# A two-layer decoder trunk on one core: new order of the mixer's steps, token halves in turn at the head of the first feed forward, and the S5 phase tables built on another engine

## The chip, the cores and the metric

The kernel runs on one core of a Trainium2 chip. The metric is the device time of the program in microseconds (us), the median over runs. The engines are named as in the profile: PE (TensorE matmuls; PEld its weight loads), DVE (VectorE), ACT (ScalarE), POOL (GpSimd), SP (SyncE, which here only issues transfers).

## The reference, cut to what matters

```python
D_MODEL, SEQ, D_FF = 1024, 1024, 4096          # one batch, float32
for i in range(2):
    h = h + mix_fns[i](rms_norm(h, norm_mix[i]), *mix_params[i])   # 0: RWKV-7 + short conv, 1: S5
    h = h + sqrelu_mlp(rms_norm(h, norm_ffn[i]), *ffn[i])          # square(relu(hn @ up)) @ down
    gate = jax.nn.sigmoid(rms_norm(h, norm_ple[i]) @ ple[i][0])
    h = h + (p[i] @ ple[i][1]) * gate
return rms_norm(h, norm_final)

# S5 (layer 1): 64 groups of 16 channels, 64 complex states a group
step = exp(log_step)[:, None]; lam_bar = exp(lam * step)           # lam complex
b_bar = ((lam_bar - 1) / lam)[..., None] * (b_re + 1j * b_im)
# h_t = lam_bar * h_(t-1) + b_bar u_t ;  y_t = Re(c h_t) + d_skip * u_t, then gelu and a GLU
```

The kernel's S5 works on chunks of tokens, so it needs powers of `lam_bar` up to 127 (the "phases", real and imaginary part, 128 states x 128 powers for each pair of groups) and products of powers with `b_bar` and `c`.

## The kernel before, in words

All activations are held transposed: 8 blocks `j` of 128 model dimensions by 1024 tokens, the tokens in two halves `hf` of 512. Every float32 product is made of three matmuls (`mm3`, L162 to L164): each operand is split into a rounded high part and the rest (`whi`/`wlo` and `uwh`/`uwl` for weights, `prh`/`prl` for inputs, `hidh`/`hidl` for hidden values), and PE adds high x high, low x high and high x low.

The stages follow each other: mixer 0 (0 to 721 us in the profiled execution), a passage to feed forward 0 (721 to 770), feed forward 0 (to 1490), the per-layer embedding (to 1614), S5 with its GLU (to 1905), feed forward 1 (to 2580), embedding and last norm (to 2722).

**Order.** PE runs in the order in which the program is written. The other engines' order is set by a scheduler from the same program, so an instruction moved in the code can move other engines' rows too. SP issues nearly all weight loads in its own order; a store placed there stands between two loads.

**Mixer 0** (`mixer0_run`, `go`). Short chains with little work per step (`f` the projections' elementwise part with `ps_w`, `ps_a`; `a`, `c` and `g` the recurrence in chunks, with `ps_Kt`, `ps_Bt`, `ps_Vt`, `ps_u`, and its output `ps_yt`) are advanced by a step, and between the steps `go` places units of long matmul work: `z` (input projection), `C` (convolution), `W` (output projection, `ps_wo`), `X` (inputs of the second half). `MIX_STEPS`, `MIX_UNITS` and `MIX_JOBS` are the tables that set who runs when. A chain's step is marked by a `yield`.

**Passage.** `done(j, hf)` splits an input tile into `prh` (ACT, L179) and `prl` (DVE, L180) and squares it for the norm (ACT `sq`, POOL `acc` L201); the norm's scale is made by `ps_ms`, a root, a reciprocal (L222) and `ps_rs`. All 16 inputs are issued ahead of feed forward 0.

**Feed forward** (`ffn`). A block `k` has 8 steps; `at(k, s, f)` puts a function at a step. In a block PE runs a down product in seven parts (`d_run`, a Strassen-like scheme with outputs `ps_dnx`, `ps_dny`, `ps_dnz`) and one up weight tile (`u_run`). `FFN_D` and `FFN_U` say at which steps of a block the weights are loaded and split: for down weights, POOL makes four sums (`draw`, L276 to L279), ACT the high part (`whi`), DVE the rest (`wlo`, L286); for up weights, ACT makes `uwh` (L260) and POOL `uwl` (L263). The raw tiles `uraw` and `draw` share two buffers. DVE adds each product to `h` or `ha` (L360). The eight up tiles of input rows j 0 to 3 and j 4 to 7 alternate (`q, b = m // 2 % 2, m % 2`).

**S5 tables under feed forward 0** (`hook`). While PE works on blocks 1 to 60, `s5_piece` makes for each of 32 pairs of groups `CL` (three POOL instructions), `BL` (three DVE instructions), two PE transposes `ps_bl`, four PE matmuls `ps_k`, and stores them; `CL`, `tmp`, `BL` and `tmp3` share one tag of four buffers (`s5b`). `s5_phases` builds the phases by doubling: seven steps, each with scaled copies on ACT (L1170) and two POOL instructions (L1171, L1172), for two pairs at a time, and POOL issues the stores (L1176).

Of the kernel before, what the change touches and what calls it, by code (L numbers as in the profile page):

```python
# [12 lines left out]
P = 128  # L13
# [7 lines left out]
S5_START, S5_PREP, S5_AT, S5_EACH = -38, 2, 36, 14  # L21
S5_FRONT = (-20, -6, -4, -3)
S5_STEPS = (0, 2, 4, 7, 10)
S5_PH = (1, 5, 9, 13, 17, 21, 25)
# [3 lines left out]
FFN_D = (0, 0, 3, 7)  # L28
# [4 lines left out]
MIX_STEPS = [14, 14, 5, 6, 8]  # L33
MIX_UNITS = [19, 48, 64, 72, 72, 48, 40, 48, 40, 40, 24]
MIX_JOBS = ['z1 C0', 'z2 C1 W45a', 'z3 C2 X3', 'N M L z4 W01a', 'z5 C4', 'z6 W23a', 'z7 C5 S', 'R C6 W45b', 'W01b C7', 'W2b W67b W3b', '']
# [25 lines left out]
class Trunk:  # L61
# [175 lines left out]
    def ffn(self, l, xn, rstd, done, hook):  # L237
# [12 lines left out]

        def u_load(m):
            c, q, b = m // 4, m // 2 % 2, m % 2
# [35 lines left out]
        def u_run(k):  # L288
# [302 lines left out]
    def rwkv_f(self, st, p, cx):  # L591
# [16 lines left out]
        nc.vector.tensor_tensor_scan(L, self.reset, sw, 0.0, ALU.mult, ALU.add)  # L608
        ps = self.pc.tile([P, H], F32, tag="a", name="ps_a")
# [28 lines left out]
    def rwkv_a(self, st, p, cx):  # L638
# [15 lines left out]
        nc.vector.scalar_tensor_tensor(RA[:, 1], v8(kk), -1.0, eL[:, :, 0:64], ALU.mult, ALU.mult)  # L654
        yield
# [40 lines left out]
    def rwkv_c(self, p, cx):  # L696
# [22 lines left out]
        self.by_token(flat(kb[:, 0]), K, "Kt")  # L719
        self.by_token(flat(kb[:, 1]), B, "Bt")  # L720
# [57 lines left out]
    def rwkv_g(self, p, cx, out):  # L778
# [20 lines left out]
        yield  # L799
# [84 lines left out]
    def s5_tables(self, pool, sp, keep_p):  # L884
# [125 lines left out]
        self.Fi = t("Fi", (2, 64), sp)  # L1010
# [6 lines left out]
        stt(self.Fi[:, 0], u, sgn, inv, MUL)  # L1017
        V.tensor_scalar_mul(self.Fi[:, 1], self.Fi[:, 0], -1.0)
# [47 lines left out]
    def s5_front(self, n, pool):  # L1066
# [37 lines left out]
    def s5_piece(self, pc, pool):
# [9 lines left out]
        X, Bb, sk = self.eight  # L1114
# [35 lines left out]
        G.tensor_add(kt[:, :, 112:128], kt[:, :, 112:128], sk[:, q])  # L1150
# [4 lines left out]
        nc.scalar.dma_start(dst, kt.rearrange("p g k -> p (g k)"))  # L1155
        yield

    def s5_phases(self, pc, pool):
# [3 lines left out]
        E = pool.tile([P, 2, 2, P], F32, tag="s5p", name="phase", bufs=1)  # L1162
        G.memset(E[:, :, 0, 0:1], 1.0)
        G.memset(E[:, :, 1, 0:1], 0.0)
        for k in range(7):
            m = 1 << k
            t = pool.tile([P, 2, 2, 64], F32, tag="s5q", name="pt", bufs=1)
            for j in range(2):
                for o, n in ((E[:, j, :, m:2 * m], 0), (t[:, j, :, :m], 1)):
                    nc.scalar.activation(o, E[:, j, :, 0:m], AF.Copy, scale=self.wk[:, k, n, pc + j:pc + j + 1])  # L1170
            G.tensor_sub(E[:, :, 0, m:2 * m], E[:, :, 0, m:2 * m], t[:, :, 1, :m])  # L1171
            G.tensor_add(E[:, :, 1, m:2 * m], E[:, :, 1, m:2 * m], t[:, :, 0, :m])  # L1172
            if k > 0:
                yield
        for j in range(2):
# [536 lines left out]
```

## Time and profile before

| | us |
|---|---|
| median of 3 runs (lowest, highest) | 2727.71 (2727.67, 2731.49) |
| the profiled execution | 2723.54 |
| its span, first to last instruction | 2721.8 |

| engine | busy us | share of the span |
|---|---|---|
| PE | 2571.1 | 94% |
| DVE | 1860.5 | 68% |
| ACT | 1078.4 | 40% |
| POOL | 1140.2 | 42% |

The shares are means over stages with different limits: a wait counts only where PE, the engine that is busy nearly all the time, waits behind it. The mean granted clock of PE was 0.982 of full speed. A matmul of 128x512 columns starts 0.23 us after the one before it at full clock and 0.43 us where the clock is at its lower level, though each one's own duration reads longer since they overlap.

### The profile page before, as it was taken

What the parts mean: (1) busy time and instruction counts of PE and PEld (TensorE: products, weight loads), DVE (VectorE), ACT (ScalarE), POOL (GpSimd) and SP (SyncE); (2) the same over time, 40 slices, a digit from 0 to 9 for tenths busy, and PEclk for the clock granted to TensorE, in tenths of its full rate; (3) what the DMA queues carried; (4) which work ended last, traced back from release to release, by engine and by line L of the source; (5) the groups of instructions that cost most, each with busy time, mean ns of one, the idle gap of its engine ahead of it and who ended that gap; (6) DMA issues with size and microseconds to landing.
All of it is one profiled execution on the core that took longest, in us unless ns stands there. A gap on an engine that the chain in (4) does not pass through costs nothing.

```text
span 2721.8 us, 47184 instructions
## 1 busy us (share of the span) xinstructions
PE 2571.1 (94%) x18781; PEld 2058.4 (76%) x18781; DVE 1860.5 (68%) x2685; ACT 1078.4 (40%) x2083; POOL 1140.2 (42%) x1524
## 2 busy tenths in 40 slices
PE   6999999989799999999999997999999999999998
PEld 5777777767577777777777876788788888888786
DVE  6655666553887787787888559423577787777854
ACT  4334444443345555533334336313323233233432
POOL 5434343443356766754545007311344334343400
PEclk9999999999899999999999989999999999999999
DMA  4213221321222332222222225211111111111121
GB/s 106 63 56 97 94 62 41 110 68 56 76 64 66 87 88 77 82 83 72 77 73 78 64 74 161 72 51 39 47 51 51 51 52 50 55 47 55 49 72 62
DMA packets 270361, 189.07 MB, mean 69 GB/s; under 512 B 33039, under 2 KB 252413, under 8 KB 270141
## 3 DMA queue, kind: packets, MB, share of 16 engines
q1 hardware_dynamic: 246160, 158.24, 19.5%
q10 hardware_dynamic: 21084, 19.17, 2.7%
q0 software_dynamic: 2896, 8.65, 0.9%
q8 instruction: 147, 2.41, 0.4%
q14 instruction: 74, 0.60, 0.1%
HBM read 156.92 MB, written 29.10 MB: 68 GB/s over the span
## 4 chain that ended last, share of the span: by engine, by line
PE 67%; DVE 13%; POOL 7%; issue 5%; ACT 4%; DMA 4%; SPq 0%; ACTq 0%; POOLq 0%; DVEq 0%
PE ps_dnx L357 9%; PE ps_up L164 6%; PE ps_up L162 6%; PE ps_up L163 6%; PE ps_dny L357 4%; PE ps_z L162 3%; PE ps_z L163 3%; PE ps_z L164 2%; PE ps_gl L162 2%; PE ps_gl L163 2%; PE ps_gl L164 2%; PE ps_g L164 2%; PE ps_g L162 2%; PE ps_g L163 2%; PE ps_dnz L357 2%
## 5 line engine op out<-in xcount | busy, mean ns | idle before, releaser
L162 PE MATMUL ps_up<-prh,uwh 128*128 128x512 f32 x1024 | 405.4, 396 | 3.6 <-ACT uwh L260 3.6
L164 PE MATMUL ps_up<-prh,uwl 128*128 128x512 f32 x1024 | 405.8, 396 | 2.8 <-POOL uwl L263 2.8
L163 PE MATMUL ps_up<-prl,uwh 128*128 128x512 f32 x1024 | 403.5, 394 | 0.0
L263 POOL TENSOR_TENSOR uwl<-uraw,uwh 128x512 fp32r<-128x512 f32 x136 | 183.2, 1347 | 189.0 <-ACT uwh L260 188.5
L357 PE MATMUL ps_dnx<-hidh,whi 128*128 128x512 f32 x480 | 196.8, 410 | 37.1 <-DVE ha L360 28.2
L164 PEld LDWEIGHTS ps_up<-prh,uwl 128*128 128x128 f32 x1024 | 193.5, 189 | 48.8 <-POOL uwl L263 3.7
L162 PEld LDWEIGHTS ps_up<-prh,uwh 128*128 128x128 f32 x1024 | 193.6, 189 | 48.5 <-ACT uwh L260 4.0
L276 POOL TENSOR_TENSOR draw<-draw 128x128 f32<-128x128 f32 x120 | 64.8, 540 | 388.4 <-DMA draw<-in_l_ffn_down_dram 356.3
L163 PEld LDWEIGHTS ps_up<-prl,uwh 128*128 128x128 f32 x1024 | 193.4, 189 | 45.0
L151 POOL TENSOR_TENSOR wlo<-wraw,whi 128x1024 fp32r<-128x1024 f32 x66 | 160.1, 2426 | 133.0 <-ACT whi L150 129.5
L360 DVE TENSOR_TENSOR h<-h,ps_dnx 128x512 f32<-128x512 f32 x240 | 164.1, 684 | 72.1 <-PE ps_dnx L357 71.2
L201 POOL TENSOR_TENSOR acc<-acc,sq 128x512 f32<-128x512 f32 x70 | 104.8, 1504 | 211.9 <-ACT sq L200 210.8
L357 PE MATMUL ps_dnx<-hidl,whi 128*128 128x512 f32 x480 | 188.8, 393 | 2.8 <-DVE hidl L322 2.8
L260 ACT CAST uwh<-uraw 128x512 fp32r<-128x512 f32 x136 | 84.0, 619 | 267.5 <-PE ps_up L163 239.5
L357 PE MATMUL ps_dnx<-hidh,wlo 128*128 128x512 f32 x480 | 189.0, 394 | 0.3 <-DVE wlo L286 0.3
L150 ACT CAST whi<-wraw 128x1024 fp32r<-128x1024 f32 x104 | 108.8, 1047 | 186.7 <-PE ps_z L163 70.3
L360 DVE TENSOR_TENSOR ha<-ha,ps_dnx 128x512 f32<-128x512 f32 x240 | 163.5, 681 | 22.4 <-PE ps_dnx L357 22.2
L162 PE MATMUL ps_z<-prh,whi 128*128 128x512 f32 x416 | 176.2, 424 | 0.3 <-ACT prh L482 0.2
L322 DVE TENSOR_TENSOR hidl<-r_up,hidh 128x512 fp32r<-128x512 f32 x188 | 152.0, 821 | 27.3 <-ACT r_up L318 20.3
L164 PE MATMUL ps_z<-prh,wlo 128*128 128x512 f32 x416 | 163.7, 393 | 1.7 <-POOL wlo L151 1.7
L163 PE MATMUL ps_z<-prl,whi 128*128 128x512 f32 x416 | 164.4, 395 | 0.9 <-DVE prl L483 0.8
L317 ACT ACTIVATE hidh<-r_up 128x512 fp32r<-128x512 f32 x98 | 61.9, 631 | 241.4 <-DVE r_up L314 229.6
(438 smaller groups left out, 6438.6 us busy)
## 6 DMA issues: line engine op xcount, KB each, us to landing
uraw<-in_l_ffn_up_dram SPq DMA_DIRECT2D x128, 256.0 KB
draw<-in_l_ffn_down_dram SPq DMA_DIRECT2D x120, 256.0 KB
wraw<-in_l_w_in_dram SPq DMA_DIRECT2D x52, 512.0 KB
s5w<-s5w SPq DMA_DIRECT2D x32, 384.0 KB
wraw<-in_l_w_out_dram SPq DMA_DIRECT2D x16, 512.0 KB
wraw<-in_l_ple_gate_dram SPq DMA_DIRECT2D x16, 512.0 KB
wraw<-in_l_glu_w_dram SPq DMA_DIRECT2D x16, 512.0 KB
toep<-kt ACTq DMA_DIRECT2D x32, 240.0 KB
```

What stands on the lines that cost most here:

```text
L150: nc.scalar.copy(hi[:, :n], raw[:, :n])
L151: self.lo_engine().tensor_sub(lo[:, :n], raw[:, :n], hi[:, :n].bitcast(F32))
L162: nc.tensor.matmul(ps, wh, xh, start=start, stop=False)
L163: nc.tensor.matmul(ps, wh, xl, start=False, stop=False)
L164: nc.tensor.matmul(ps, wl, xh, start=False, stop=stop)
L201: (eng or nc.vector).tensor_add(acc, acc, sq)
L260: A.copy(uw[m][0], raws["u"])
L263: nc.gpsimd.tensor_sub(uw[m][1], raws["u"], uw[m][0].bitcast(F32))
L276: G.tensor_add(raw[:, 4], raw[:, 0], raw[:, 2])
L322: return lambda: eng.tensor_sub(st[nm][1], t, st[nm][0].bitcast(F32))
L357: nc.tensor.matmul(ps, w[:, a], v, start=id(ps) not in begun, stop=n == 2, skip_group_check=True)
L360: V.tensor_add(hv, hv, ps)
```

## The change

- **Mixer.** New tables; the units start with `z` work ahead of `ps_w` and `ps_a`; a step boundary stands between `ps_w` and `ps_a`, between `ps_Kt` and `ps_Bt`, and two more ahead of `ps_yt`; the norm of a half is asked for three steps later; the second half's inputs are transposed one job ahead.
- **Passage.** `part(m)` orders the first four up tiles so that tiles 0 and 1 need only the inputs j 0 to 3, of both halves, and tiles 2 and 3 those of j 4 to 7. Inputs are put into feed forward 0's due table (block -6, step 2), behind the split of the first weights; the mean square and the scale of the norm come at later steps (blocks -5 and -4).
- **Down weights.** `FFN_D` goes from (0, 0, 3, 7) to (0, 2, 5, 7): the high part two steps later, the low part two steps later.
- **Pieces of S5.** Own buffers for `CL`, `tmp`, `BL`, `tmp3`, `brep`; stores of `CL` and `kt` issued by SP instead of ACT; the skip term `sk` per piece.
- **Phases.** Power k = 8a + b is made as a product of two short tables: `s5_powers` builds tables of 8 and 16 powers for 8 pairs at once (7 steps of 4 small POOL instructions), and `s5_phases` multiplies them out per pair: two POOL products of 256 columns, a difference and a sum of 128; SP issues the store. ACT has no part in it. The phase has one buffer.
- The pieces start at step 88 instead of 36 and come every 12 steps instead of 14.

```diff
-S5_START, S5_PREP, S5_AT, S5_EACH = -38, 2, 36, 14
-S5_PH = (1, 5, 9, 13, 17, 21, 25)
+S5_START, S5_PREP, S5_AT, S5_EACH = -24, 1, 88, 12
+S5_PH = (1, 2, 4)
-FFN_D = (0, 0, 3, 7)
+FFN_D = (0, 2, 5, 7)
-MIX_UNITS = [19, 48, 64, 72, 72, 48, 40, 48, 40, 40, 24]
+MIX_UNITS = [8, 48, 64, 72, 72, 48, 40, 48, 40, 40, 24]
...
+        def part(m):
+            return (m % 2, m // 2) if m < 4 else (m // 2 % 2, m % 2)
...
         self.by_token(flat(kb[:, 0]), K, "Kt")
+        yield
         self.by_token(flat(kb[:, 1]), B, "Bt")
...
-        big = lambda nm: pool.tile([P, NG, 9, 16], F32, tag="s5b", name=nm, bufs=4)
+        big = lambda nm, k: pool.tile([P, NG, k, 16], F32, tag=nm, name=nm, bufs=1)
...
-            nc.scalar.dma_start(W[:, 128 * NG:256 * NG].rearrange("(g p) (r k) -> r p g k", g=NG, r=2)[r],
+            nc.sync.dma_start(W[:, 128 * NG:256 * NG].rearrange("(g p) (r k) -> r p g k", g=NG, r=2)[r],
...
     def s5_phases(self, pc, pool):
-        for k in range(7):
-            m = 1 << k
-            t = pool.tile([P, 2, 2, 64], F32, tag="s5q", name="pt", bufs=1)
-            for j in range(2):
-                for o, n in ((E[:, j, :, m:2 * m], 0), (t[:, j, :, :m], 1)):
-                    nc.scalar.activation(o, E[:, j, :, 0:m], AF.Copy, scale=self.wk[:, k, n, pc + j:pc + j + 1])
-            G.tensor_sub(E[:, :, 0, m:2 * m], E[:, :, 0, m:2 * m], t[:, :, 1, :m])
-            G.tensor_add(E[:, :, 1, m:2 * m], E[:, :, 1, m:2 * m], t[:, :, 0, :m])
-            nc.gpsimd.dma_start(self.s5w[pc + j][:, 256 * NG:384 * NG], E[:, j].rearrange("p n c -> p (n c)"))
+        E = pool.tile([P, 2, 16, 8], F32, tag="s5p", name="phase", bufs=1)
+        G.tensor_mul(E, hi, lo(0))
+        G.tensor_mul(t, hi, lo(1))
+        G.tensor_sub(E[:, 0], E[:, 0], t[:, 1])
+        G.tensor_add(E[:, 1], E[:, 1], t[:, 0])
+        nc.sync.dma_start(self.s5w[pc][:, 256 * NG:384 * NG], E.rearrange("p n a b -> p (n a b)"))
...
+                        def hook(at, ffn_in=st, ffn_done=done):
+                            at(-6, 2, lambda: inputs(ffn_in, ffn_done))
+                            at(-5, 6, lambda: next(ffn_in["r"]))
+                            at(-4, 4, lambda: scale1(ffn_in))
```

How the rows of three engines move (each row: line, operation, output, inputs, shape; lines of the changed kernel are a few higher). PE at the start of the mixer, where `ps_w` and `ps_a` read `tw`, which ACT makes from the first projection; before:

```order
L164 MATMUL ps_z<-prh,wlo 128x512
L228 MATMUL ps_rs<-ident,rs_413 128x128 x4
L162 MATMUL ps_z<-prh,whi 128x512
L163 MATMUL ps_z<-prl,whi 128x512
L164 MATMUL ps_z<-prh,wlo 128x512
L602 MATMUL ps_w<-tw,lwa 128x512
L610 MATMUL ps_a<-tw,lwa 128x512
L162 MATMUL ps_z<-prh,whi 128x512
```

and now, 25 matmul rows behind `ps_rs`:

```order
L163 MATMUL ps_z<-prh,whi 128x512
L164 MATMUL ps_z<-prl,whi 128x512
L165 MATMUL ps_z<-prh,wlo 128x512
L607 MATMUL ps_w<-tw,lwa 128x512
L163 MATMUL ps_z<-prh,whi 128x512
L164 MATMUL ps_z<-prl,whi 128x512
L165 MATMUL ps_z<-prh,wlo 128x512
L163 MATMUL ps_z<-prh,whi 128x512
L164 MATMUL ps_z<-prl,whi 128x512
L165 MATMUL ps_z<-prh,wlo 128x512
L616 MATMUL ps_a<-tw,lwa 128x512
```

`ps_w` has moved behind projection work that stood after it, and `ps_a` follows two products later. PE in the passage, behind the first up products (`ps_up`); before, nine of them stand ahead of the norm (`ps_ms`, `ps_rs`) and of the tables' transposes (`ps_lam`):

```order
L164 MATMUL ps_up<-prh,uwl 128x512
L218 MATMUL ps_ms<-meanw,acc 128x1 x4
L228 MATMUL ps_rs<-ident,rs_8946 128x128 x4
L915 MATMUL ps_lam<-ident,lraw_l_lambda_re 128x64
L915 MATMUL ps_lam<-ident,lraw_l_lambda_im 128x64
L915 MATMUL ps_lam<-ident,lraw_d 128x64
L162 MATMUL ps_up<-prh,uwh 128x512
```

and now 24 stand ahead of `ps_ms`, and 25 more between it and this piece:

```order
L165 MATMUL ps_up<-prh,uwl 128x512
L229 MATMUL ps_rs<-ident,rs_9026 128x128 x4
L163 MATMUL ps_up<-prh,uwh 128x512
L164 MATMUL ps_up<-prl,uwh 128x512
L165 MATMUL ps_up<-prh,uwl 128x512
L924 MATMUL ps_lam<-ident,lraw_l_lambda_re 128x64
```

The norm has moved behind the first two weight tiles. POOL in feed forward 0, a stretch of one block; before, from the end of one phase pair to the start of the next:

```order
L263 TENSOR_TENSOR uwl<-uraw,uwh 128x512
L1171 TENSOR_TENSOR phase<-phase,pt 128x2x64
L1172 TENSOR_TENSOR phase<-phase,pt 128x2x64
L1176 DMA s5w_63<-phase 128x256
L1176 DMA s5w_64<-phase 128x256
L328 TENSOR_TENSOR r_up<-r_up 128x512
L276 TENSOR_TENSOR draw<-draw 128x128
L277 TENSOR_TENSOR draw<-draw 128x128
L1163 MEMSET phase 128x2
```

and now, where three phases stand close together:

```order
L268 TENSOR_TENSOR uwl<-uraw,uwh 128x512
L1200 TENSOR_TENSOR pt<-E_10248,E_10247 128x256
L1199 TENSOR_TENSOR phase<-E_10248,E_10247 128x256
L1202 TENSOR_TENSOR phase<-phase,pt 128x128
L1203 TENSOR_TENSOR phase<-phase,pt 128x128
L1200 TENSOR_TENSOR pt<-E_10248,E_10247 128x256
L1199 TENSOR_TENSOR phase<-E_10248,E_10247 128x256
L1202 TENSOR_TENSOR phase<-phase,pt 128x128
L1203 TENSOR_TENSOR phase<-phase,pt 128x128
L281 TENSOR_TENSOR draw<-draw 128x128
```

In POOL's new order the rows of blocks 4 to 22 (from one set of `draw` rows to the next is a block) hold all 32 phases (128 rows), 112 small rows of the short tables, 7 of the 32 `CL` pieces, 19 `uwl`, 76 `draw` and 10 rows of hidden values. The other 25 pieces lie in the later blocks. Before, the same blocks held 64 rows each of L1171 and L1172, 20 stores, 10 pieces and the same weights and hidden values.

## Rows read from the trace of the kernel before

**Rows 1.** The page: busy time of each engine with its share of the span and its instructions.

```profile
PE 2571.1 (94%) x18781; PEld 2058.4 (76%) x18781; DVE 1860.5 (68%) x2685; ACT 1078.4 (40%) x2083; POOL 1140.2 (42%) x1524
```

**Rows 2.** Busy time by stretch. Columns: the stretch and its length, busy us and instructions of PE, PEld, DVE, ACT and POOL, then PE's granted clock, the share of the DMA engines and GB/s. 811.7 to 1037.1 is from the first `ps_dnz` product of block 4 to that of block 23, 1037.1 to 1464.4 from there to block 60's, 2000 to 2100 lies in feed forward 1.

```profile
0.00:60.00 60.00, 40.99 (x178) 30.68 (x179) 33.92 (x45) 27.78 (x38) 29.34 (x43) 0.94 0.44 110
60.00:721.00 661.00, 624.67 (x9792) 491.63 (x9791) 400.09 (x574) 267.37 (x491) 267.85 (x264) 0.98 0.24 74
721.00:760.00 39.00, 26.45 (x98) 20.45 (x97) 36.46 (x118) 16.54 (x29) 15.95 (x12) 0.74 0.10 28
811.70:1037.10 225.40, 209.11 (x923) 166.00 (x921) 180.20 (x259) 127.18 (x378) 155.47 (x315) 1.00 0.29 81
1037.10:1464.40 427.30, 409.36 (x1802) 326.66 (x1801) 343.52 (x509) 170.41 (x384) 239.33 (x380) 0.99 0.28 78
2000.00:2100.00 100.00, 100.00 (x434) 81.23 (x434) 76.85 (x108) 31.74 (x47) 38.41 (x51) 1.00 0.17 53
```

**Rows 3.** PE's waits in the mixer, 60 to 721 us: who waits for whom, us in total, times, the longest.

```profile
PE ps_u L710 <- ACT gsq L806: 6.3, 7, 1.8
PE ps_Vt L691 <- ACT Kt L694: 6.3, 2, 4.9
PE ps_wo L162 <- DVE h L587: 4.1, 6, 2.0
PE ps_ms L218 <- POOL acc L201: 3.5, 1, 3.5
```

**Rows 4.** The timeline of PE at the start of the mixer: start, duration, engine, line, operation, and in brackets the idle time before it and its releaser.

```profile
46.06 1.22 PE L602 MATMUL ps_w<-tw,lwa 64*128 64x512 f32 x1 [5.46 <-ACT tw L520]
...
49.08 0.63 PE L164 MATMUL ps_z<-prh,wlo 128*128 128x512 f32 x1
...
50.50 0.40 PE L162 MATMUL ps_z<-prh,whi 128*128 128x512 f32 x1
```

**Rows 5.** The timeline of the passage, DVE and PE.

```profile
722.74 6.13 DVE L180 SCALAR_TENSOR_TENSOR prl<-h,cv,prh 128x512 fp32r<-128x512 f32 x4
...
725.42 0.50 PE L162 MATMUL ps_up<-prh,uwh 128*128 128x512 f32 x1 [3.61 <-ACT uwh L260]
...
728.37 0.79 PE L164 MATMUL ps_up<-prh,uwl 128*128 128x512 f32 x1 [2.19 <-POOL uwl L263]
...
733.43 1.86 PE L218 MATMUL ps_ms<-meanw,acc 128*128 128x1 f32 x8 [1.71 <-POOL acc L201]
...
737.16 2.73 DVE L180 SCALAR_TENSOR_TENSOR prl<-ha,cv,prh 128x512 fp32r<-128x512 f32 x4
...
740.03 2.08 PE L228 MATMUL ps_rs<-ident,rs 128*128 128x128 f32 x8 [4.73 <-DVE rs L222]
...
743.12 0.79 PE L162 MATMUL ps_up<-prh,uwh 128*128 128x512 f32 x1
...
746.60 0.40 PE L164 MATMUL ps_up<-prh,uwl 128*128 128x512 f32 x1
```

**Rows 6.** The timeline of PE in feed forward 1 (first product into `ps_dnz` of two blocks in turn), and PE's waits in feed forward 0, 800 to 1490 us.

```profile
2044.65 0.39 PE L357 MATMUL ps_dnz<-hidh,whi 128*128 128x512 f32 x1
...
2055.05 0.39 PE L357 MATMUL ps_dnz<-hidh,whi 128*128 128x512 f32 x1
...
PE ps_dnx L357 <- DVE ha L360: 26.8, 29, 2.3
PE ps_dnx L357 <- DVE h L360: 6.7, 5, 2.0
```

**Rows 7.** POOL's groups of instructions in blocks 4 to 22 of feed forward 0: line, operation, tiles, shape, count, busy us and mean ns, idle time before and its releasers. Last, the transfers of the finished phases: issuing queue, count, size, median us from issue to landing.

```profile
L1171 POOL TENSOR_TENSOR phase<-phase,pt 128x128 f32<-128x128 f32 (+6 forms) x64 | 22.0, 344 | 28.9 <-ACT pt L1170 26.1 <-PE ps_up L164 1.5 <-PE ps_dnx L357 0.8
L1172 POOL TENSOR_TENSOR phase<-phase,pt 128x128 f32<-128x128 f32 (+6 forms) x64 | 19.8, 310 | 0.0
L1176 POOL DMA_DIRECT2D s5w<-phase x20 | 11.4, 571 | 1.5 <-POOL phase L1172 1.5
L1123 POOL TENSOR_TENSOR CL<-CL,tmp 128x288 f32<-128x288 f32 x11 | 10.6, 959 | 0.2
L277 POOL TENSOR_TENSOR draw<-draw 128x128 f32<-128x128 f32 x19 | 10.1, 531 | 0.0
...
L1120 POOL TENSOR_TENSOR CL<-LR,cx 128x288 f32<-128x288 f32 x11 | 9.4, 851 | 2.4 <-PE ps_bl L1138 1.7 <-ACT cx L1088 0.6
L1121 POOL TENSOR_TENSOR tmp<-LI,cx 128x288 f32<-128x288 f32 x11 | 7.5, 678 | 1.3 <-PE ps_dny L357 1.0 <-DMA s5w<-bi 0.2
...
s5w<-phase POOLq DMA_DIRECT2D x32, 128.0 KB, 2.1
```

**Rows 8.** DVE's groups in the same blocks, and the scaled copies into `phase` on ACT over feed forward 0 (as many again, 69.6 us, go into `pt`).

```profile
L322 DVE TENSOR_TENSOR hidl<-r_up,hidh 128x512 fp32r<-128x512 f32 x29 | 24.8, 870 | 9.2 <-ACT r_up L318 8.5
L286 DVE TENSOR_TENSOR wlo<-draw,whi 128x896 fp32r<-128x896 f32 x19 | 23.7, 1246 | 6.0 <-ACT whi L283 5.2 <-POOL phase L1172 0.9
L328 DVE TENSOR_TENSOR r_up<-r_up 128x512 f32<-128x512 f32 x15 | 16.2, 1080 | 1.6 <-ACT r_up L318 1.6
...
L1170 ACT ACTIVATE phase<-phase,wk 128x2 f32<-128x2 f32 (+6 forms) x224 | 71.0, 317 | 69.7 <-POOL phase L1172 47.4 <-POOL phase L1164 21.5 <-ACT r_up L318 0.2
```

**Rows 9.** The timeline of one block of feed forward 0, DVE and PE.

```profile
860.17 2.38 DVE L328 TENSOR_TENSOR r_up<-r_up 128x512 f32<-128x512 f32 x1
...
863.80 0.49 PE L357 MATMUL ps_dnx<-hidh,whi 128*128 128x512 f32 x1 [2.34 <-DVE ha L360]
```

More of the change, by code (lines that the diff above doesn't have):

```diff
@@ L249, in at @@
             due.setdefault(8 * k + s, []).append(f)
+        def part(m):
+            return (m % 2, m // 2) if m < 4 else (m // 2 % 2, m % 2)
         def u_load(m):
-            c, q, b = m // 4, m // 2 % 2, m % 2
+            c, (q, b) = m // 4, part(m)
             ap = (up[b * 512:(b + 1) * 512, c * 256 + q * P:c * 256 + (q + 1) * P].rearrange("(k p) c -> p k c", p=P) if m < NU
@@ L294, in u_run @@
                 return
-            q, b, st = m // 2 % 2, m % 2, sts[m // 4]
+            (q, b), st = part(m), sts[m // 4]
             first = (1, 0) if m < 4 else (0, 1)
@@ L654, in rwkv_a @@
         nc.vector.scalar_tensor_tensor(RA[:, 1], v8(kk), -1.0, eL[:, :, 0:64], ALU.mult, ALU.mult)
+        yield
         yield
@@ L719, in rwkv_c @@
         self.by_token(flat(kb[:, 0]), K, "Kt")
+        yield
         self.by_token(flat(kb[:, 1]), B, "Bt")
@@ L798, in rwkv_g @@
         nc.vector.tensor_mul(Yv, Yv, bc(s2))
-        yield
+        for _ in range(3):
+            yield
         ps = self.pc.tile([P, H], F32, tag="b", name="ps_yt")
@@ L1009, in s5_tables @@
         V.tensor_mul(self.Fr, u, inv)
-        self.Fi = t("Fi", (2, 64), sp)
+        self.Fi = t("Fi", where=sp)
         V.tensor_mul(u, ni, lre)
@@ L1154, in s5_piece, with s5_powers @@
         dst = bass.AP(ap.tensor, ap.offset, [[16 * R - 16, 8], [R, 16], [1, 240 * NG]])
-        nc.scalar.dma_start(dst, kt.rearrange("p g k -> p (g k)"))
+        nc.sync.dma_start(dst, kt.rearrange("p g k -> p (g k)"))
         yield
+    def s5_powers(self, n, pool):
+        G = self.nc.gpsimd
+        E1 = pool.tile([P, 8, 2, 8], F32, tag="E1", name="E1", bufs=1)
+        E2 = pool.tile([P, 8, 2, 16], F32, tag="E2", name="E2", bufs=1)
+        self.pw = E1, E2
+        ks = slice(8 * n, 8 * n + 8)
+        for k in range(7):
+            E, m = (E1, 1 << k) if k < 3 else (E2, 1 << k - 3)
+            if m == 1:
+                G.memset(E[:, :, 0, 0:1], 1.0)
+                G.memset(E[:, :, 1, 0:1], 0.0)
+            t = pool.tile([P, 8, 2, 8], F32, tag="pt", name="pq", bufs=1)[:, :, :, :m]
+            w = lambda c: self.wk[:, k, c, ks].rearrange("p (q o e) -> p q o e", o=1, e=1).broadcast_to([P, 8, 2, m])
+            old, new = E[:, :, :, 0:m], E[:, :, :, m:2 * m]
+            G.tensor_mul(new, old, w(0))
+            G.tensor_mul(t, old, w(1))
+            G.tensor_sub(new[:, :, 0], new[:, :, 0], t[:, :, 1])
+            G.tensor_add(new[:, :, 1], new[:, :, 1], t[:, :, 0])
+            yield
     def s5_phases(self, pc, pool):
@@ L1401, in go @@
             jobs = list(jobs)
-            nstep = max([c[1] for c in crit], default=1)
+            nstep = max([c[1] + (c[2] if len(c) > 2 else 0) for c in crit], default=1)
             later = [c for c in crit if len(c) > 2]
@@ L1463, in scale @@
         def scale(st):
-            yield
+            for _ in range(3):
+                yield
             r = self.rstd_steps(st["acc"], pool=self.pc, tag="a")
@@ L1484, in mixer0_run, with ahead, rest @@
         X = lambda hf, s: [self.m0_x(hf, j, s) for j in range(ND)]
+        def ahead(js):
+            def rest(q):
+                yield
+                yield from q
+            next(js[0])
+            return [rest(js[0])] + js[1:]
         def mix(a, b, n):
@@ L1510, in mixer0_run @@
         pre = pre[:1] + pre[2:3] + pre[1:2] + pre[3:]
-        for q in xs[:1]:
+        for q in xs[:1] + pre[:1] + xs[1:3] + pre[1:2] + xs[3:]:
             next(q)
-        for q in pre[:2]:
+        for q in xs[:1] + pre[:1] + xs[1:3] + pre[1:2]:
             next(q)
-        for q in xs[1:]:
-            next(q)
-        for q in xs[:2]:
-            next(q)
-        for q in xs[2:]:
-            next(q)
-            for o in pre[:2]:
-                next(o)
-        for _ in range(2):
-            for o in pre[:2]:
+        for q in xs[3:] + [None] * 2:
+            for o in ([q] if q else []) + pre[:2]:
                 next(o)
@@ L1529, in mixer0_run @@
         r = scale(A)
-        next(r)
+        for _ in range(3):
+            next(r)
         for _ in range(4):
@@ L1581, in build @@
             nc.sync.dma_start(r0, self.rscr)
-            st, done = self.prep("l0_norm_ffn", eng=nc.gpsimd, known={0: r0})
+            st, done = self.prep("l0_norm_ffn", eng=nc.gpsimd, known={0: r0}, late=True)
             s5p = E(tc.tile_pool(name="s5p", bufs=1, reuse_waits="tile"))
@@ L1585, in build @@
                 return self.dump()
-            for js in range(0, 4), range(4, 8):
-                for hf in (1, 0):
-                    for j in js:
-                        done(j, hf)
             for l in range(2):
@@ L1619, in build, with inputs, scale1 @@
                         next(tab)
-                        def hook(at):
+                        def inputs(ffn_in, ffn_done):
+                            for js in range(0, 4), range(4, 8):
+                                for hf in (1, 0):
+                                    for j in js:
+                                        ffn_done(j, hf)
+                            r = ffn_in["r"] = self.rstd_steps(ffn_in["acc"][1])
+                        def scale1(ffn_in):
+                            ffn_in["rstd"][1] = next(ffn_in["r"])[0]
+                        def hook(at, ffn_in=st, ffn_done=done):
+                            at(-6, 2, lambda: inputs(ffn_in, ffn_done))
+                            at(-5, 6, lambda: next(ffn_in["r"]))
+                            at(-4, 4, lambda: scale1(ffn_in))
                             def start(s):
```

86 lines of the change are left out of this document (45 added, 41 removed).

## The prediction, made before the changed kernel ran

> **What bounds the kernel now.** I read the page, then busy time by stretch, then PE's waits stage by stage, then the timeline where a wait is long. PE is busy 94% of the span [rows 1], so the time is PE's work plus PE's waits, and the stretches tell where those are [rows 2]: 661.0 - 624.7 = 36 us in the mixer, 12.5 us in the 39 us passage (at a granted clock of 0.74), 16 us in blocks 4 to 22 of feed forward 0, 18 us in blocks 23 to 59, and nothing in feed forward 1, where PE is at 100%. That last stretch is the measure of feed forward 0: there a block takes 2055.05 - 2044.65 = 10.4 us [rows 6]; in feed forward 0 it takes 225.4 / 19 = 11.86 us in blocks 4 to 22 and 427.3 / 37 = 11.55 us later [rows 2]. PE waits there nearly always for DVE's additions to `ha` and `h`, 26.8 and 6.7 us [rows 6]. DVE is not slow by itself: it stands behind others. In the block shown one `r_up` took 2.38 us [rows 9], where the group's mean is 1.08 [rows 8], beside a busy POOL, and PE then waited 2.34 us; `hidl` and `wlo` wait 8.5 and 5.2 us for ACT [rows 8]. ACT has 448 scaled copies for the phases in its queue (71.0 + 69.6 us), in turn with POOL: ACT waits 47.4 us for POOL [rows 8] and POOL 26.1 us for ACT [rows 7].
>
> **Start of the mixer.** `ps_w` waits 5.46 us for ACT's `tw`, and the matmuls behind it run long (0.63 us against 0.40) until 50.5 [rows 4]. Now `ps_w` stands behind 24 more products of ready inputs: 24 x 0.23 = 5.5 us of work in the place of the wait. Bounds: 0, if their weights are not there in time (the first weights come through ACT and POOL too), and -7 (the wait and the slow stretch). I take **-3**.
>
> **Mixer.** No work is added. The waits that the new order bears on are `ps_Vt` for the copies of `Kt` (6.3 us; `ps_Bt` now stands apart, so the copies get some products' time), `ps_ms` for POOL's `acc` (3.5; three steps later), `ps_u` for `gsq` (6.3; `ps_yt` later) and `ps_wo` for `h` (4.1) [rows 3]: 20.2 us. Against that, products used as cover at one place are missing at another. Bounds: +10, if they are missed at as many places as they help (half of 20), and -16. I take **-8**.
>
> **Passage.** Before, PE starts up products at 725.42, waits 2.19 us for `uwl`, 1.71 for the norm's `acc` and 4.73 for the reciprocal, which on DVE stands behind all the `prl` until 739.9, and takes up products again at 743.12; at 746.60 it starts the eighteenth (nine before the norm, eight from 743.12 on) [rows 5]. Now 24 stand ahead of `ps_ms` and 48 ahead of `ps_rs`, and they need only the first eight `prl`, done by half of DVE's stretch (about 734). By 746.6 PE could have done 53 or so: 24 as inputs come until 735, the rest at 0.23 to 0.43 us. 36 more at 0.235 us: **-8.5** (bounds -4, if POOL, whose `acc` and `uwl` now alternate, gives the second `uwl` late, and -12). The tables' DVE work moves under blocks 1 to 3, which I leave at 0: their DVE load then comes near PE's.
>
> **Blocks 4 to 22.** ACT loses all its copies, 127 us busy of 225 before [rows 2]. PE's need is 19 x 10.4 = 198 us and the narrow products of 7 pieces, an estimate of 0.7 us each (six products at half the time of a wide one), 5 us: 203. But POOL now has all 32 phases and all powers in these blocks. Its sum: before 155.5 us [rows 2], less phases 22.0 + 19.8, stores 11.4 and pieces 10.6 + 9.4 + 7.5 [rows 7] leaves 74.8 for weights and hidden values. Added: pieces 7/11 of 27.5 = 17.5; a phase is two products of 256 columns, 0.68 us each (L1121 and L1120 have 288 columns at 0.678 and 0.851, mean 0.76, times 256/288), and two rows of 128 at 0.53 (L277): 2.42 x 32 = 77.4; powers 112 x 0.327 (mean of L1171 and L1172 over widths 2 to 128) = 36.6 [rows 7]. Together 206 us, about PE's need. On top, a phase's first write into its single buffer waits until the last store has landed, 2.1 us after issue on the old queue [rows 7]; about half of the phases have other POOL work in between, so 16 x 1.3 = 20 us. POOL enters ahead of PE (a down weight's sums are made a block, 10.4 us, before use, of which split and rest use some 4), so 6 us of this is free: 206 + 20 - 6 = 220 to 221. Against 225.4: **-4**. Bounds: 203 (-22), POOL free of contention and waits; 246 (+21), each phase waiting and no lead.
>
> The row that speaks against this part: a DVE instruction with two SBUF inputs is held while POOL works (2.38 us, [rows 9]). If POOL's 206 and DVE's `hidl` and `wlo`, 24.8 + 23.7 us [rows 8], took strict turns, these blocks would take 255; but both durations already hold time blocked by the other, so I count the middle of 206 and 255, 230, plus waits, into the first rival. The Trainium skill says in "SBUF — State Buffer", section "SBUF: two separate sides", that DVE and GpSimd lock a shared port pair for a whole instruction and the loser blocks; the trace agrees with 2.38 us for that `r_up`, and by that rule alone the sum would end about 34 us higher than by the forecast, near no change.
>
> **Down weights later** (`FFN_D`): ACT's `whi` and DVE's `wlo` no longer head their queues while POOL's sums run: `wlo` waited 5.2 us for `whi` [rows 8], part of the gains here. `wlo` is due at step 5 and used at the next block's start, 3 steps of 1.3 us; it takes 1.25 us, so I cost this at 0. If DVE is 2.7 us late there, PE waits for it.
>
> **Blocks 23 to 59.** No phases on any engine; own buffers for `BL` and `CL` end waits of `BL` for POOL, and 64 issues move from ACT to SP. PE's need is 37 x 10.4 + 25 x 0.7 = 402; before 427.3, so at most 25 us. POOL has about 6 us a block there. As blocks behind the phases in the old kernel still had waits, I take half: **-12** (bounds -4 and -22).
>
> **Other stages**: same work, 0.
>
> **Sum.** -3 - 8 - 8.5 - 4 - 12 = -35.5 on the profiled execution's 2723.5: 2688. The median lies 4.2 us above that execution, so 2692.
>
> **Rivals.**
> - *POOL over-full.* Phases cost POOL what ACT saved: blocks 4 to 22 at 239 (230 and 9 of waits), +14 instead of -4, so -17.5: 2710. For it: POOL's sum equals PE's need with no room. Against it: POOL waited 28.9 us for ACT in these blocks, which goes [rows 7]. Chance 0.20.
> - *Slower, by the store's way round.* SP issues in order, and phase stores stand between weight loads: SP waits for POOL's phase, POOL for the store and for the load behind it. Slower begins where these blocks pass 225.4 + 31.5 (what the other terms win) + 5.5 = 262, which on POOL's 206 is a mean wait of 1.8 us for each of 32 phases. With 2.5 us (the store's 2.1 [rows 7] and 0.4 for the load behind it) they take 286: +61 - 31.5, or 2757. Against it: loads run a block ahead. Chance 0.08.
> - *No change that can be measured.* The mixer's new order misses cover elsewhere (+10) while POOL is over-full (+14): -3 + 10 - 8.5 + 14 - 12 = +0.5, or 2728; strict turns of POOL and DVE, 255 (+30), with the mixer as forecast, end at -1.5, or 2726. Chance 0.08.
> - *More.* Contention fades when the ping-pong ends: blocks 4 to 22 at 203, later ones -20, mixer -16: -69.5, 2658. Chance 0.10.
> - The forecast, 2676 to 2706: 0.54.
>
> **Numbers.** A change within 0.2% (5.5 us) can't be told from none. Faster: 0.54 + 0.20 + 0.10 = 0.84; same 0.08; slower 0.08. The range 2666 to 2722 leaves out the slower case, most of the unchanged one and a part of the largest gain.
>
> **What would show it.** Right: the wait of `ps_w` gone; `ps_rs` later with no wait; the passage's stretch with up products and a clock near full sooner; ACT's busy time in blocks 4 to 22 well below 127 us; POOL near 90% there; PE's waits for `ha` less. Wrong, above all, if POOL waits for `s5w` stores or `draw` loads in blocks 4 to 22 and PE for `uwl` or `wlo`, or if the mixer's total idle stays at 36 us with other names.

## The result, and the profile after

The changed kernel takes 2732.45 us (median of 20 runs, 2728.82 to 2738.2) against 2727.72 for the kernel before on the same chip; the ratio is 1.0018, interval [1.0011, 1.0025]. The interval lies above 1, but the 4.7 us are less than the 5.5 us that the prediction counts as no change. Forecast were 2692 us and a range of 2666 to 2722, so the result lies outside it. The profiled execution took 2731.33 us, its span 2729.6.

Stretches, from the starts of the last row of `ps_wo` and of each block's first row of `ps_dnz` in both traces (us). The two profiled executions lie 7.8 us apart, the medians 4.7, since the one of the kernel before lay 4.2 below its median:

| stretch | before | after | change | forecast |
|---|---|---|---|---|
| to the last output product of the mixer | 721.4 | 717.7 | -3.7 | -11 |
| from there to block 1's `ps_dnz` | 55.0 | 40.7 | -14.3 | |
| blocks 1 to 3 | 35.3 | 44.3 | +9.0 | |
| (both together) | | | -5.3 | -8.5 |
| blocks 4 to 22 | 225.4 | 238.9 | +13.5 | -4 |
| blocks 23 to 59 | 427.3 | 430.7 | +3.4 | -12 |
| all behind | | | 0 | 0 |

Busy time up to the mixer's last output product, before and after, columns as in [rows 2]:

```profile
0.00:721.40 721.40, 666.05 (x9969) 522.65 (x9970) 434.41 (x619) 295.44 (x530) 297.59 (x306) 0.97 0.26 77
0.00:717.70 717.70, 674.34 (x9970) 526.35 (x9970) 427.30 (x619) 296.09 (x530) 297.47 (x306) 0.97 0.26 78
```

The other stretches of the changed kernel:

```profile
60.00:721.00 661.00, 628.91 (x9782) 492.30 (x9780) 396.78 (x580) 270.41 (x497) 270.50 (x267) 0.97 0.24 74
721.00:758.45 37.45, 35.16 (x144) 26.29 (x144) 34.30 (x89) 17.79 (x31) 19.67 (x15) 0.92 0.15 43
758.45:802.77 44.32, 35.99 (x137) 27.62 (x136) 41.18 (x101) 11.68 (x18) 23.63 (x54) 0.85 0.21 50
802.77:1041.70 238.93, 215.42 (x903) 170.32 (x902) 185.75 (x253) 68.93 (x114) 208.72 (x370) 0.96 0.27 78
1041.70:1472.40 430.70, 412.46 (x1829) 330.89 (x1828) 357.41 (x517) 142.24 (x255) 220.40 (x320) 0.99 0.28 77
```

ACT's load fell as told (127 to 69 us in blocks 4 to 22) and POOL's came out as summed (208.7, forecast 206). Yet PE lost time there twice: it waits 23.5 us instead of 16.3, and it is busy 215.4 us instead of 209.1, with a granted clock of 0.96 where it was 1.00. PE's waits in blocks 4 to 22, then ACT's wait for the down weights' sums and POOL's phase groups there:

```profile
PE ps_dnx L362 <- DVE ha L365: 16.2, 10, 3.3
PE ps_dnx L362 <- DVE h L365: 7.3, 3, 3.7
...
ACT whi L288 <- POOL draw L284: 34.9, 13, 4.8
...
L1200 POOL TENSOR_TENSOR pt<-E,E 128x256 f32<-128x256 f32 x32 | 23.6, 739 | 0.9
L1199 POOL TENSOR_TENSOR phase<-E,E 128x256 f32<-128x256 f32 x32 | 22.3, 696 | 9.1 <-DMA s5w<-phase 8.2 <-PE ps_up L165 0.8
L1202 POOL TENSOR_TENSOR phase<-phase,pt 128x128 f32<-128x128 f32 x32 | 21.0, 656 | 0.8
L1203 POOL TENSOR_TENSOR phase<-phase,pt 128x128 f32<-128x128 f32 x32 | 16.6, 519 | 0.0
```

ACT waited 7.1 us for `draw` before (`whi`, L283, three times). How such a wait reaches PE, in one block (timeline, several engines):

```profile
937.17 0.46 POOL L284 TENSOR_TENSOR draw<-draw 128x128 f32<-128x128 f32 x1
...
937.66 0.94 ACT L288 CAST whi<-draw 128x896 fp32r<-128x896 f32 x1 [3.86 <-POOL draw L284]
...
938.63 2.00 DVE L291 TENSOR_TENSOR wlo<-draw,whi 128x896 fp32r<-128x896 f32 x1 [1.13 <-ACT whi L288]
...
940.56 0.67 DVE L365 TENSOR_TENSOR ha<-ha,ps_dnx 128x512 f32<-128x512 f32 x1
...
941.29 0.50 PE L362 MATMUL ps_dnx<-hidh,whi 128*128 128x512 f32 x1 [3.29 <-DVE ha L365]
```

The last of the four sums stands on POOL between phase rows; ACT's `whi` waits for it, DVE's `wlo` for ACT, and `wlo`, 1.25 us in the mean of [rows 8], takes 2.00, with POOL's `uwl` running beside it; the addition to `ha`, whose product PE had finished by 938.0, stands behind `wlo` on DVE, and PE behind the addition. And what a long wait costs beyond itself (PE's timeline at another such place):

```profile
905.80 0.79 PE L362 MATMUL ps_dnx<-hidh,whi 128*128 128x512 f32 x1 [3.19 <-DVE ha L365]
906.39 0.63 PE L362 MATMUL ps_dnx<-hidl,whi 128*128 128x512 f32 x1
...
911.08 0.60 PE L362 MATMUL ps_dny<-hidh,whi 128*128 128x512 f32 x1
911.51 0.40 PE L362 MATMUL ps_dny<-hidl,whi 128*128 128x512 f32 x1
```

The thirteen matmuls that start from 905.80 to 911.08 are 0.43 us apart (the first 0.59) instead of 0.23: the clock is at its lower level (0.50 from 904.7 to 911.5), and 2.7 us go on top of the 3.19. The waits before, no longer than 2.34 us, left the clock of blocks 4 to 22 at 1.00 [rows 2]; four of the new ones, of 2.1 to 3.7 us, were followed by such stretches. The length of a wait alone does not decide it: one of 2.14 us was followed by six slow matmuls, the one of 2.34 before by none.

### The profile page after: what moved, and what is told of

It reads as the page before. It is cut to its first block, busy times and chain, and to the rows that moved or that the text cites. A ratio compares the mean times of both kernels' runs of the same rounds, so it can differ in the third digit from the quotient of the medians.

```text
span 2729.6 us, 46656 instructions
## 1 busy us (share of the span) xinstructions
PE 2589.0 (95%) x18781; PEld 2068.6 (76%) x18781; DVE 1873.7 (69%) x2684; ACT 980.3 (36%) x1635; POOL 1172.6 (43%) x1516
## 4 chain that ended last, share of the span: by engine, by line
PE 51%; DVE 6%; POOL 6%; issue 3%; DMA 1%; ACT 1%; POOLq 0%; SPq 0%; ACTq 0%; DVEq 0%
PE ps_dnx L362 10%; PE ps_up L163 6%; PE ps_up L165 6%; PE ps_up L164 6%; PE ps_dny L362 5%; PE ps_dnz L362 2%; PE ps_gl L163 2%; PE ps_gl L164 2%; PE ps_gl L165 2%; PE ps_g L163 2%; PE ps_g L165 2%; PE ps_g L164 2%; DVE ha L365 1%; POOL zs L1276 1%; DVE hidl L327 1%
## 5 line engine op out<-in xcount | busy, mean ns | idle before, releaser
L202 POOL TENSOR_TENSOR acc<-acc,sq 128x512 f32<-128x512 f32 x70 | 105.0, 1507 | 220.8 <-ACT sq L201 217.7
```

Source lines behind the costliest of these rows:

```text
L202: (eng or nc.vector).tensor_add(acc, acc, sq)
```

## Experiments

All are timed against the kernel before on the same chip (its medians there 2726.9 to 2729.2). The ratios are as on record, some of them up to 0.0013 from the quotient of the two medians. Stretches are read from one profiled execution of each run.

**Without the phases' work.**

```diff
-        G.tensor_mul(E, hi, lo(0)) ...
+        G.memset(E, 0.0)
-                                    gs.append((lazy(self.s5_powers, n // 8), S5_POW))
```

> The changed kernel without the powers and products of the phases: a phase is one clearing on POOL and its store, so the phases' content is left out. Theory A, POOL over-full: the phases that run ahead in blocks 4 to 22 hold up the down weights' sums, so without them these blocks fall from 238.9 us to 210 to 215 and the whole to about 2708. Theory B, it is not the phases but the later splitting of the down weights, or the stores in SP's queue (which stay here): blocks 4 to 22 stay within 5 us of 238.9 and the whole at 2728 to 2733.

2705.38 us, ratio 0.9908 [0.989, 0.9925]; blocks 4 to 22 take 213.9 us, blocks 23 to 59 431.6. Theory A: the phases cost 25 us, all in these blocks. The store of each phase stayed in SP's queue, so it is not the stores. The busy times of blocks 4 to 22, and ACT's wait for the sums:

```profile
802.40:1016.30 213.90, 206.75 (x903) 165.68 (x902) 175.15 (x250) 68.42 (x114) 110.19 (x173) 0.99 0.30 85
...
ACT whi L288 <- POOL draw L284: 9.8, 6, 2.8
```

**The old phases in the changed kernel.**

```diff
-        G.tensor_mul(E, hi, lo(0)) ...
+                    nc.scalar.activation(o, E[:, j, :, 0:m], AF.Copy, scale=self.wk[:, k, n, pc + j:pc + j + 1]) ...
+S5_PH = (1, 4, 8, 11, 14, 18, 21)
```

> The changed kernel with the phases made as before, by doubling on ACT and POOL, at the new places (a pair of groups every 24 steps). Theory A: POOL keeps about 1.4 us less a phase and is held to ACT's pace, the phases are spread over more blocks; blocks 4 to 22 at 215 to 226, later blocks some us longer, the whole 2718 to 2726. Theory B: blocks 4 to 22 within 5 us of 238.9, the whole 2730 or more.

2717.1 us, ratio 0.9954 [0.9939, 0.997]: blocks 4 to 22 at 220.0. Among the versions that compute everything, this one and two that move the phases into the embedding (below, ratios 0.9964 and 0.9945) are the fastest; all three are faster than both kernels. Against the run without phases, the old phases cost 6 us in blocks 4 to 22, where two thirds of their rows stand (71 of 112 differences on POOL), and 11.7 of the median; the new ones cost 25 there and 26 of the median.

**The new phases in the kernel before.**

```diff
-            for j in range(2): ... nc.scalar.activation(...)
+        G.tensor_mul(E, hi, lo(0)) ...
-        w = pool.tile([P, 8, 16], F32, tag="bw", name="w", bufs=1)
+        w = pool.tile([P, 8, 16], F32, tag="s5b", name="w", bufs=4)
```

> The kernel before with the phases alone made from two short tables (at the old places; one scratch tile shares a buffer to make room). Theory A: blocks 4 to 22 go from 225.4 us to 235 to 240 and the whole to 2735 to 2742. Theory B: no slower than before, 2715 to 2728, since ACT's 448 copies go.

2736.65 us, 1.0029 [1.0018, 1.004]; blocks 4 to 22 at 240.6. The short tables alone, with their stores on SP, turn 225.4 into 240.6, the upper end of theory A.

**POOL in the program's order.**

```diff
-                    with tc.manual_schedule(engines={mybir.EngineType.PE}):
+                    with tc.manual_schedule(engines={mybir.EngineType.PE, mybir.EngineType.Pool} if l == 0 else {mybir.EngineType.PE}):
```

> The changed kernel with POOL's rows in feed forward 0 in the order of the program instead of the scheduler's: the same rows, but a phase every 12 steps over blocks 11 to 59 instead of all 32 by block 22. Theory A: blocks 4 to 22 fall to 208 to 218, later blocks grow by at most 10, the whole 2708 to 2720 (the passage may lose some us, since the second uwl then stands behind all the squares' sums). Theory B: blocks 4 to 22 stay above 230.

2736.96 us, 1.003 [1.0017, 1.0043]: blocks 4 to 22 at 222.2, but the later ones at 445.3, and the passage up to block 1 took 8.9 us more than in the changed kernel. Neither theory holds. The miss has two parts in feed forward 0 that this run can't separate: the phases moved later, and POOL now stands still in front of rows that the scheduler had put elsewhere, and with it the hidden values behind them (POOL's waits, blocks 4 to 59):

```profile
POOL kt L1160 <- issue: 115.1, 24, 9.8
POOL r_up L333 <- ACT r_up L323: 58.6, 11, 12.9
```

**Phases spread by a shared buffer.**

```diff
-        t = pool.tile([P, 2, 16, 8], F32, tag="pt", name="pt", bufs=1)
+        t = pool.tile([P, 2, 16, 8], F32, tag="tmp", name="pt", bufs=1)
```

> The changed kernel with the phases' scratch tile in the same single buffer as a scratch tile of the pieces, which alone spreads the phases over blocks 11 to 59, one beside each piece, in the scheduler's order. Theory A1, the queue: POOL then has room in every block (about 9 of 11 us), blocks 4 to 22 at 214 to 221, later blocks at most 8 us more than 430.7, the whole 2712 to 2722. Theory A2, contention: the cost of about 25 us moves with the rows; blocks 4 to 22 at 218 to 224, later ones at 442 to 450, the whole 2727 to 2735.

2728.19 us, 0.9993 [0.9983, 1.0002]. In its profiled execution, the fastest of its ten, blocks 4 to 22 take 214.8 and the later ones 444.2, where 24 of the 32 phases now stand: the cost moved with the rows. In that execution it is about half of the 25 us, but the median lies 9.3 us higher. Spreading them wins little, as A2 told; POOL having room in a block is not enough.

**Clearings in the place of the phases.** Seven, then eleven, clearings for a phase (the edit shows the second form).

```diff
-        G.tensor_mul(E, hi, lo(0)) ...
+        for _ in range(6):
+            G.memset(E, 0.0)
```

> The changed kernel with every row of the powers and phases replaced by clearings on POOL of about the same length (seven of 0.28 us for a phase, 28 of 0.2 us for a set of powers), so that POOL is as long occupied but reads nothing; the phases' content is left out. Theory A1, the queue: what counts is that POOL gets to the down weights' sums later; blocks 4 to 22 at 230 to 239 us and the whole at 2724 to 2733. Theory A2, contention: what counts is that POOL's reads hold DVE's instructions with two SBUF inputs; blocks 4 to 22 at 214 to 222 and the whole at 2705 to 2714.

2715.47 us, 0.9949 [0.9934, 0.9963]; blocks 4 to 22 at 220.8, within A2's range, and the whole just above it; but POOL was busy for only 172 us there.

> As the run with cleared phases, with more clearings (eleven for a phase, 42 for a set of powers), so that POOL is busy for about 205 us in blocks 4 to 22 as in the changed kernel (208.7), again without reading; the phases' content is left out. Theory A1, the queue alone: blocks 4 to 22 back at 233 to 240 us, the whole 2726 to 2733. Theory A2, contention by reads: they stay at 220 to 227, the whole 2714 to 2720.

2718.28 us, 0.9957 [0.9942, 0.9972]: 216.7 and, later, 438.5. A1's numbers fail, and A2's hold for the whole only. But POOL was again not as full as meant: 187 us in blocks 4 to 22, since a third of the clearings went into later blocks. Its added work over blocks 4 to 59 is 109 us, more than the 99 that the phases added, and costs 10.6 us of the median where the phases cost 26.3 (each median taken against the kernel before on its own chip).

Two things differ between the runs in blocks 4 to 22. DVE is busy 175.2 us without phases, 174.0 with clearings and 185.8 with phases, in 250, 252 and 253 instructions: only POOL's reading rows lengthened DVE's time as a whole (single groups move either way: `wlo` takes 1336 ns in the mean with clearings, 1230 without phases). And ACT waits 9.8, 9.9 and 34.9 us for the sums: the scheduler placed the clearings so that the sums were not late. So the run does not divide the cost between late sums and reads; that split stays open. The rows:

```profile
805.54:1022.23 216.69, 207.14 (x903) 165.54 (x902) 173.98 (x252) 67.42 (x113) 187.12 (x530) 0.99 0.26 77
ACT whi L288 <- POOL draw L284: 9.9, 5, 4.0
L291 DVE TENSOR_TENSOR wlo<-draw,whi 128x896 fp32r<-128x896 f32 x19 | 25.4, 1336 | 4.9 <-ACT whi L288 4.7
```

(cleared, blocks 4 to 22) and, in the changed kernel:

```profile
L291 DVE TENSOR_TENSOR wlo<-draw,whi 128x896 fp32r<-128x896 f32 x19 | 28.8, 1517 | 11.0 <-ACT whi L288 10.8
```

**Phases in the embedding.** Three forms: all on POOL; every third on DVE; half on DVE and none before the embedding's first scale.

```diff
-                        self.ple(l, st2["xn"], rstd, pt, done1, [])
+                            side = [ph] * (64 // NG)
+                        self.ple(l, st2["xn"], rstd, pt, done1, side)
...
+        G = nc.vector if pc % 3 == 2 else nc.gpsimd
```

> The changed kernel with all phases and powers moved behind feed forward 0, into the per-layer embedding that follows, where POOL is busy 12 of 124 us (three phase buffers). Theory A, both kinds: feed forward 0 as without phases (blocks 4 to 22 at 214), the embedding at most 4 us longer, the whole 2704 to 2712. Rival: the phases' stores in SP's queue hold up the embedding's loads, or S5 has to wait for the last of them: the whole 2716 to 2730.

2718.81 us, 0.9964 [0.995, 0.9978]. Feed forward 0 won 25 us, and 15 came back at the way into S5, as the rival told: ACT stood 11.03 us in front of one of S5's first rows until a phase's store was done, and the root of S5's norm, for which PE waits through DVE's `rs`, stands behind that row on ACT. That S5's tile takes the place of the phases' scratch is the likely reason; no run shows it.

```profile
1611.86 0.51 ACT L1247 ACTIVATE rc<-later,rho 128x256 f32<-128x256 f32 x1 [11.03 <-DMA s5w<-phase]
...
PE ps_rs L229 <- DVE rs L223: 12.1, 2, 10.9
```

> The phases in the embedding as before, but every third of them made by DVE, which is busy 68 of 124 us there. Theory: the run with all of them on POOL lost about 11 us because the last phase ended 10 us after the embedding's products and S5's scratch space and scale waited for it; with 22 phases on POOL the last ends before, S5 starts at once, and the whole is at 2704 to 2711. Rival: the loss is in the stores among SP's loads or in DVE's rows, and the whole stays at 2716 or more.

2715.57 us, 0.9945 [0.9926, 0.9964]: that wait is gone, but the theory's total is missed: the stretch to the GLU is still 13 us longer than in the changed kernel, with a lower clock in it. The profiled execution was the slowest of its five.

> The phases in the embedding, half of them on DVE, and none before the embedding's first scale is there (the first power reads it), so that POOL's squares for that scale are not held up. Theory: the split run still waited 2.5 us for these squares, and its clock then fell; without that the embedding and S5 take the 256 us of the changed kernel, the whole 2704 to 2711. Rival: the stores among SP's loads or the rows on DVE cost the same wherever they stand: 2714 to 2719.

2724.82 us, 0.9986 [0.9975, 0.9997]: now PE waits 10.6 us for DVE's squares. Both ranges are missed. In all three forms phases close to a stage's end delayed what the next stage starts from, whichever engine made them.

**Down weights split as before.**

```diff
-FFN_D = (0, 2, 5, 7)
+FFN_D = (0, 0, 3, 7)
```

> The changed kernel with the down weights split as early as before, FFN_D = (0, 0, 3, 7). Theory A: this part is free, the whole within 4 us of 2732. Rival: with POOL full, the later split is what lets wlo come too late; the whole 2718 to 2727 and blocks 4 to 22 below 233.

2733.66 us, 1.0015 [1.0003, 1.0026]; blocks 4 to 22 at 238.7: free, as forecast.

**The old mixer.**

```diff
-MIX_UNITS = [8, 48, 64, 72, 72, 48, 40, 48, 40, 40, 24]
+MIX_UNITS = [19, 48, 64, 72, 72, 48, 40, 48, 40, 40, 24]
```

(and the other tables and step boundaries of the mixer as before)

> The changed kernel with the mixer's steps and tables of before. Theory M: the new mixer order is worth the 3.7 us by which the last output product ends earlier, no more: the whole 2733 to 2738, the last ps_wo at 721 to 722. Rival: the new order costs time elsewhere, or nothing: the whole within 1.5 us of 2732 or below.

2737.27 us, 1.0033 [1.002, 1.0045]: the new order is worth 3 to 5 us of the whole (1.0033 against 1.0018, or 4.8 by the medians), as theory M told, though the last `ps_wo` starts at 723.6.

**Later tables.**

```diff
-S5_START, S5_PREP, S5_AT, S5_EACH = -24, 1, 88, 12
+S5_START, S5_PREP, S5_AT, S5_EACH = -8, 1, 96, 12
```

> The changed kernel with the tables' steps two blocks later (and the pieces one block later). Theory T: block 1 takes 22.4 us because the tables' small DVE rows stand among its split and difference rows; block 1 falls below 17, blocks 1 to 3 below 39, the first ps_dnz stays at 758 to 760, the whole 2724 to 2729. Rival: block 1 is long by the first weights and hidden values themselves, which come two halves at once: blocks 1 to 3 stay at 42 to 45.

2730.65 us, 1.0002 [0.9989, 1.0016]. Block 1 falls from 22.4 to 16.5 us, but blocks 1 to 3 only from 44.3 to 41.3, and the whole does not move beyond the noise: theory T holds for block 1 alone. The tables' rows cost time where they stand.

**Pieces made lighter**, both without the phases' work.

```diff
-        V.tensor_mul(BL, bcc(LR[:, :, 0:8], 8), bck(Bb[0], 8)) ... (three rows)
+        V.memset(BL, 0.0)
```

> The changed kernel without the phases' content (as in the first run) and with DVE's three BL instructions of a piece replaced by one clearing (BL's content is left out too). Theory D, DVE is the bound of the later blocks: it is busy 357 of 430.7 us there, its BL rows with their blocked time some 44 us; without them blocks 23 to 59 fall from 431.6 to 408 to 416 us and the whole to 2682 to 2692. Theory P, POOL's CL rows beside DVE are the cause: 424 to 432.

2683.94 us, 0.9839 [0.9811, 0.9867]: blocks 23 to 59 from 431.6 to 412.9, with PE's clock at 1.00. DVE was the bound, as theory D told.

```diff
-        G.tensor_mul(CL, bcc(LR, 9), bck(X[0], 9)) ... (three rows)
+        G.memset(CL, 0.0)
```

> The changed kernel without the phases' content and with POOL's three CL instructions of a piece replaced by one clearing (CL's content is left out). Theory P: blocks 23 to 59 fall to 408 to 418. Theory D: POOL has room there and only its held time on DVE goes: 422 to 430, the whole 2696 to 2704.

2692.49 us, 0.9865 [0.9835, 0.9895]: 422.0. POOL's rows cost half as much, with POOL busy 220 of 431 us. What they did to DVE is in the rows of blocks 23 to 59 without phases, then also without `BL`, then without phases and `CL`:

```profile
1016.30:1447.80 431.50, 412.22 (x1828) 331.03 (x1827) 357.53 (x517) 142.31 (x255) 219.94 (x320) 0.99 0.28 77
1011.29:1424.19 412.90, 407.86 (x1828) 329.21 (x1827) 327.37 (x470) 142.73 (x255) 225.38 (x320) 1.00 0.30 81
1013.72:1435.67 421.95, 409.74 (x1828) 330.04 (x1827) 342.45 (x517) 142.20 (x255) 167.93 (x272) 0.99 0.29 79
```

Without `CL` DVE does the same 517 instructions in 342.5 us instead of 357.5, while POOL is busy 52 us less: its reading rows had held DVE for 15 us. In both runs the stretch shrinks by a little over 0.6 us for each us that DVE is less busy (18.7 for 30.2, 9.6 for 15.1). So it is not a full queue, but DVE's time.

## Why the prediction was wrong, by its own steps

- **Start and mixer, -11: the waits fell as told, the time did not.** `ps_w`'s wait is gone, `ps_Vt`'s went from 6.3 to 2.1, and PE's idle time up to the last output product fell from 55.3 to 43.4 us, although new waits for weights (`ps_z` for POOL's `wlo`, 6.5 us, up to 2.4) and for the norm (3.8) came. But PE was busy for 8.3 us longer with the same matmuls. So the step that failed here is to take a wait saved for time saved. This is no accident of two executions: the three traces with the old mixer end this stretch at 721.4 to 724.4 us with 54.4 to 55.6 idle, the fourteen with the new one at 715.0 to 720.9 with 43.4 to 46.2. Why PE is busy longer stays open. The granted clock does not settle it: over 60 to 721 us it is 0.97 in the changed kernel against 0.98, but also 0.97 in the run with the old mixer (end at 723.6) and 0.98 in the run with later tables (new mixer, end at 717.1).
- **Passage, -8.5: more than forecast until block 1, then given back.** The first block started 14.3 us sooner relative to the mixer's end, beyond the bound of -12, and blocks 1 to 3, which I left at 0 though I wrote that DVE's load came near PE's, took 9.0 more: DVE is busy 41.2 of 44.3 us there, PE waits 2.3 and 4.1 us for `hidl`, and the clock is at its lower level (0.50) from 761.4 to 774.9. Together -5.3.
- **Blocks 4 to 22, -4: the step that failed first.** POOL's sum was right (206 against 208.7), the store's wait even smaller than told (8.2 us, not 20). What failed is the step from "POOL's sum equals PE's need" to a time: an average over 19 blocks says nothing of where a weight's sums stand in a block, and the 6 us of lead that the sum set against the waits did not cover it. ACT waited 34.9 us for the sums instead of 7.1, DVE's `wlo` came later and took longer, and PE waited 7.2 us more and, at a lower clock that the sum had no term for, was busy 6.3 us more. The first rival, POOL over-full, had these blocks at 239, and 238.9 was measured (238.7 in each of the runs with the old mixer and the old split); that its number fits is in part luck, since it was made of 230 us of POOL's rows and 9 of waits, and POOL was busy for 208.7. Its chance of 0.20 was too small, and its total of 2710 failed with the other terms. The runs without phases and with the new phases in the kernel before show that the phases are the cause; how much of it is late sums and how much POOL's reads beside DVE stays open (the cleared runs).
- **Blocks 23 to 59, -12: the second step that failed.** I took half of PE's waits as won because ACT and POOL lost work. PE's waits stayed (17.9 us before, 18.2 after). DVE was the bound and got more: 357.4 us busy against 343.5, with 24 pieces in these blocks instead of 21 (the rows of both traces). The run without `BL` shows it. The +3.4 itself is no more than the noise: the runs with the old mixer and with the old split have these blocks at 427.4 and 429.6. The Trainium skill, "SBUF — State Buffer", section "SBUF: two separate sides", that a DVE instruction with two SBUF inputs and a GpSimd instruction that reads SBUF lock each other out of a shared port pair, was the warning that I counted only in part. The runs without `CL` and with clearings agree with it: DVE's rows were 15 us shorter with POOL busy 52 us less, and clearings, which read nothing, did not lengthen DVE's time. Strict turns over all of POOL's time, as in the sum's 255, did not show.
- **The slower rival** (stores in SP's queue) did not occur: POOL waited 5.9 us for `draw`'s loads in blocks 4 to 22, where it had waited 24.7 before, and the run without phases kept these stores. The whole came out near the time before by terms that failed together.

## What to carry to other kernels

Before moving work from a half-idle engine, ask which engine the critical one really waits for: here that was DVE, and freeing ACT won less than POOL's new rows cost. Sum a shared in-order engine by position, not by its total: what matters is which rows now stand ahead of the one that others wait for. Price a wait with the clock: one of 3.19 us here cost 5.9 with the slow matmuls behind it. And do not book a saved wait as saved time: in the mixer 12 us of waits went, but only 3.7 us of time.

## What the runs showed of the hardware

- A wait of 3.19 us of PE was followed by thirteen matmuls at the lower clock level, 2.7 us more; after waits of 1.2 to 1.9 us in the same blocks the pace stayed at 0.23 us.
- POOL's rows that read SBUF lengthened DVE's: 517 DVE instructions took 357.5 us beside them and 342.5 with POOL busy 52 us less. Clearings on POOL did not: DVE was busy 174.0 us beside 73 us of clearings for phases, 175.2 with 9.
